# An encoder layer with routed experts: routing in two parts, two tiles' logits in another place, slots listed at another time

## The chip, the cores and the metric

The kernel runs on one core of one Trainium2 chip. The metric is the device time in microseconds of one execution of the whole program. The core has TensorE (matmuls into PSUM; PE in the profile, its weight loads PEld), VectorE (DVE), ScalarE (ACT), GpSimd (POOL) and SyncE (SP), which run their own instruction streams in order and wait for one another by semaphores; DMAs are issued from SP and from POOL.

## The reference

One layer on 1024 tokens of width 1024: two attention mixers, an output projection, then a mixture of experts, and a last norm. What the change touches is the routing of the experts:

```python
g_logits = xt @ router_group_w + router_group_b          # 4 groups
g_prob = softmax(g_logits);  g_top_p, g_top = top_k(g_prob, 1)
e_logits = xt @ router_expert_w + router_expert_b        # 4 x 8 experts
e_in_group = e_logits of the chosen group
e_top_logit, e_top = top_k(e_in_group, 2)
gates = g_top_p * softmax(e_top_logit)
expert_id = g_top * 8 + e_top                            # two experts per token
...
for each expert e:  h[tok] += gate * ((silu(x[tok] @ w_gate[e]) * (x[tok] @ w_up[e])) @ w_down[e])
```

For each expert the kernel needs two lists: which token rows it gets, and the gate of each of them.

## The kernel before

The tokens are 8 tiles of 128. The stage of interest comes after the mixers. A loop over the tiles `j` makes the second half of the output projection: `projected(j, b)` for two halves `b` of 512 columns, 12 matmuls each (L827), and VectorE's add into `q_a` (b = 0) and `h_b` (b = 1, L964). Then ScalarE squares, GpSimd makes the reciprocal root (`rstd`, L135 and L136; of `turned` for `on` and of `projected` for `xn`), VectorE writes the normed tile `xn` (L972), and SP stores it to `xn_d`. `mixed(j)` turns the next mixer tile (`on` L814, transposes L819). The routing of a tile is a generator, `routed(j)`, of which the loop takes one step after the other between the products: two groups of transposes of the new tile (L984, copied to `xt` by ScalarE), the logits (L990) and VectorE's choice of a group and of two experts (to `ohb`, L1021), the places by a product with a triangle (L1024, L1025), then the gates and the places (L1026 to L1050), and last a product that puts both into the lists (L1054): `put` has a one where a token's place is the slot, `what` holds in 32 columns each the token's number and its gate, and `first_at` in PSUM sums over all tiles. For the tiles below `JV` = 6, GpSimd makes `put` and `what`.

When the last tile is in, VectorE turns `first_at` into `rows` (L1108) and `gate` (L1109); `load_rows` gathers the rows of expert 0 from `xn_d` into `x_g` with an indirect DMA from GpSimd (L1163), TensorE transposes them (L1180), and the experts begin: 32 of them, each with 12 weight pieces of 512 KB, which are loaded 39 ahead (`load_until`), split into a high and a low part by ScalarE (`wh`) and VectorE (`wl`), and multiplied (L1196, L1220). The rows of the next expert are gathered after the sixth piece (`KR` = 5). `listed(j)` scatters each token's number and gate to `slot_d` in DRAM with two indirect DMAs (L1062); these lists are only read where an expert has more than 128 tokens.

The order of TensorE's instructions is the order in which the code stands (`manual_schedule`); that of the other engines is set by a scheduler from when it expects operands to be ready. `issue_after(x)` holds instructions back until `x` has been placed.

## Time and profile before

| | us |
|---|---|
| three runs: lowest, median, highest | 1390.99, 1392.51, 1394.03 |
| the profiled execution | 1393.38 |
| its span, first to last instruction | 1391.7 |
| last tile's add into `h_b`; the rows are ready | 745.9; 758.2 |
| first gather issued, transposes of expert 0 begin | 758.5, 763.1 |
| second gather issued, transposes of expert 1 begin | 767.8, 776.9 |

Times in the trace are microseconds from the span's start. A table by stretches gives, for each engine, its busy time in the stretch and the number of its instructions, the share of TensorE's full clock that was granted (PEclk), the mean busy share of the 16 DMA engines and their rate. A row of the timeline gives the start, the duration, the engine, the line, and what is written and read; in brackets stands how long the engine was idle just before and what ended it.

### The profile page before, as it was taken

What the parts mean: (1) busy time and instruction counts of PE and PEld (TensorE: products, weight loads), DVE (VectorE), ACT (ScalarE), POOL (GpSimd) and SP (SyncE); (2) the same over time, 40 slices, a digit from 0 to 9 for tenths busy, and PEclk for the clock granted to TensorE, in tenths of its full rate; (3) what the DMA queues carried; (4) which work ended last, traced back from release to release, by engine and by line L of the source; (5) the groups of instructions that cost most, each with busy time, mean ns of one, the idle gap of its engine ahead of it and who ended that gap; (6) DMA issues with size and microseconds to landing.
All of it is one profiled execution on the core that took longest, in us unless ns stands there. A gap on an engine that the chain in (4) does not pass through costs nothing. (4 is left out here: it accounts for less than half of the span.)

```text
span 1391.7 us, 21904 instructions
## 1 busy us (share of the span) xinstructions
PE 1303.2 (94%) x7333; PEld 1110.6 (80%) x7333; DVE 1152.4 (83%) x2001; ACT 926.2 (67%) x1366; POOL 568.6 (41%) x556
## 2 busy tenths in 40 slices
PE   5999899999998999999897999999999999999983
PEld 5999779888976889889686788878888888888862
DVE  5788997899868777667587799989999999999976
ACT  5334556655566656556443688878888888888873
POOL 5673566745566645446354611122111111111215
PEclk9999999999998999899998999999999999999997
DMA  7113321231242564445767999999999999999925
GB/s 258 62 39 85 84 68 54 61 75 36 58 138 60 145 186 117 112 128 164 278 210 240 308 371 367 353 341 372 360 351 351 345 360 355 349 353 342 376 74 226
DMA packets 213044, 299.63 MB, mean 215 GB/s; under 512 B 94307, under 2 KB 115939, under 8 KB 212928
## 3 DMA queue, kind: packets, MB, share of 16 engines
q1 hardware_dynamic: 200528, 272.91, 58.1%
q0 software_dynamic: 11968, 24.55, 6.7%
q8 instruction: 58, 0.95, 0.3%
q10 hardware_dynamic: 432, 0.75, 0.3%
q14 instruction: 58, 0.48, 0.1%
HBM read 267.85 MB, written 44.58 MB: 224 GB/s over the span
## 5 line engine op out<-in xcount | busy, mean ns | idle before, releaser
L140 DVE TENSOR_TENSOR wl<-unit,wh 128x1024 fp32r<-128x1024 f32 x140 | 168.4, 1223 | 21.1 <-ACT wh L131 20.1
L1163 POOL DMA_INDIRECT o_b<-xn_d,rows x32 | 51.4, 1606 | 303.1 <-PE ps_a L1180 300.8
L131 ACT ACTIVATE wh<-unit 128x1024 fp32r<-128x1024 f32 x140 | 147.3, 1062 | 36.3 <-PE ps_b L1196 12.5
L529 POOL TENSOR_TENSOR psum<-psum,p 128x512 f32<-128x512 f32 x93 | 138.0, 1484 | 66.7 <-ACT p L131 56.6
L263 PE MATMUL ps_i<-wih,ul 128*128 128x256 f32 x576 | 163.1, 283 | 1.2 <-DVE ul L140 1.2
L261 PE MATMUL ps_i<-wih,uh 128*128 128x256 f32 x576 | 162.7, 283 | 0.8 <-ACT uh L131 0.8
L262 PE MATMUL ps_i<-wil,uh 128*128 128x256 f32 x576 | 162.2, 282 | 0.0
L131 ACT ACTIVATE ph<-p 128x512 fp32r<-128x512 f32 x192 | 119.0, 630 | 12.7 <-DVE pl L445 5.7
L445 DVE TENSOR_TENSOR pl<-p,ph 128x512 fp32r<-128x512 f32 x93 | 96.1, 1035 | 24.7 <-ACT ph L131 24.6
L131 ACT ACTIVATE p<-ps_b 128x512 f32<-128x512 f32 x128 | 74.6, 595 | 62.2 <-PE ps_b L519 39.7
L261 PEld LDWEIGHTS ps_i<-wih,uh 128*128 128x128 f32 x576 | 109.6, 190 | 7.0 <-ACT uh L131 1.5
L262 PEld LDWEIGHTS ps_i<-wil,uh 128*128 128x128 f32 x576 | 109.4, 190 | 5.5
L263 PEld LDWEIGHTS ps_i<-wih,ul 128*128 128x128 f32 x576 | 109.5, 190 | 5.1 <-DVE ul L140 1.7
L696 POOL TENSOR_TENSOR pl<-p,ph 128x512 fp32r<-128x512 f32 x64 | 83.4, 1309 | 73.2 <-ACT ph L131 51.9
L1233 POOL DMA_INDIRECT y_d<-y,rows x31 | 50.3, 1622 | 137.5 <-ACT y L131 134.2
L140 DVE TENSOR_TENSOR wl<-rawc,wh 128x1024 fp32r<-128x1024 f32 x70 | 84.4, 1223 | 10.4 <-ACT wh L131 9.9
L500 DVE TENSOR_REDUCE m<-ps_x 128x1 f32<-128x512 f32 x128 | 84.9, 678 | 7.9 <-PE ps_x L499 7.6
L1196 PE MATMUL ps_b<-wh,x_hi 128*128 128x512 f32 x256 | 87.0, 421 | 0.0
L131 ACT ACTIVATE wh<-rawc 128x1024 fp32r<-128x1024 f32 x70 | 74.3, 1067 | 18.2 <-PE ps_b L1196 7.2
L1220 PE MATMUL ps_d<-wh,h_hi 128*128 128x512 f32 x256 | 81.0, 397 | 1.7 <-ACT h_hi L131 1.7
L1220 PE MATMUL ps_d<-wh,h_lo 128*128 128x512 f32 x256 | 81.1, 398 | 1.5 <-DVE h_lo L140 1.5
L1196 PE MATMUL ps_c<-wh,x_hi 128*128 128x512 f32 x256 | 80.9, 397 | 0.0
(326 smaller groups left out, 3888.9 us busy)
## 6 DMA issues: line engine op xcount, KB each, us to landing
unit<-in_w_up SPq DMA_DIRECT2D x49, 512.0 KB
unit<-in_w_gate SPq DMA_DIRECT2D x47, 512.0 KB
unit<-in_w_down SPq DMA_DIRECT2D x44, 512.0 KB
rawc<-in_w_gate SPq DMA_DIRECT2D x25, 512.0 KB
rawc<-in_w_down SPq DMA_DIRECT2D x23, 512.0 KB
rawc<-in_w_up SPq DMA_DIRECT2D x22, 512.0 KB
h_b<-in_w_down SPq DMA_DIRECT2D x19, 512.0 KB
raw<-in_w_in SPq DMA_DIRECT2D x36, 256.0 KB
```

The lines of the kernel that those rows point to most:

```text
L131: A.activation(o, i, f, **kw)
L140: (eng or V).tensor_tensor(lo, src, hi, op=OP.subtract)
L261: T.matmul(ps[:, jj], u_hi[j][:, k], wh, start=(k == 0 and jj == 0), stop=False, skip_group_check=True)
L262: T.matmul(ps[:, jj], u_hi[j][:, k], wl, start=False, stop=False, skip_group_check=True)
L263: T.matmul(ps[:, jj], u_lo[j][:, k], wh, start=False, stop=(k == 7), skip_group_check=True)
L445: engine("pl").tensor_tensor(pl, p, ph, op=OP.subtract)
L500: V.tensor_reduce(m2[:, j, b:b + 1], ps, axis=AX.X, op=OP.max)
L529: engine("s").tensor_tensor(st["s"], st["s"], p, op=OP.add)
L696: G.tensor_tensor(pl, p, ph, op=OP.subtract)
L1163: gathers.append(G.indirect_dma_start(out=x_g, out_offset=None, in_=xn_d[:, :], in_offset=bass.IndirectOffsetOnAxis(ap=rows, axis=0), boun ...
L1196: T.matmul(st["gu"[n % 2]], lhs[:, k % 4], rhs[:, 512 * a:512 * a + 512], start=(k == 0 and i == 0), stop=(k == 7 and i == 2))
L1220: T.matmul(py[b], lhs[:, k], w[n][:, 512 * b:512 * b + 512], start=(k == 0 and i == 0), stop=(k == 3 and i == 2))
```

## The change

Routing is cut in two. First only what the rows need: the places, `put` and `what` with the token's number alone (now all on VectorE), and a product of 32 columns (L1051 in the new numbering). Then the gates: two `Exp`, the reciprocals, `gates` on GpSimd for the tiles below 6, and a second product of 32 columns with the same `put` (L1074). The logits of tile 6 stand inside the last product of tile 7, those of tile 7 in two halves, the first ahead of the transposes of its second half. `rows` is made as soon as the first products of tile 7 are in; the gates of tiles 6 and 7 follow after it. `listed(e - 2)` stands in the loop of the experts for e = 2 to 9, with no `issue_after` round it, and `list_blocks` moves from expert 8 to expert 10.

```diff
-            run(half_product(1, o, ps, b))
+            for k, _ in enumerate(half_product(1, o, ps, b)):
+                if k == 1 and between:
+                    between()
...
+            def logits(ks):
+                if not lp:
+                    lp.append(bank("c", [P, 36]))
+                for k in ks:
+                    T.matmul(lp[0], xt[:, k], wr[:, k], start=(k == 0), stop=(k == 7))
...
+                if j == NT - 1 and b == 0:
+                    logits(range(4))
+                    yield
+            logits(range(4 if j == NT - 1 else 0, 8))
...
             T.matmul(pc, trib, ob, start=True, stop=False)
             T.matmul(pc, oneb, cum, start=False, stop=True)
+            puts = []
+            for k in range(2):
+
+                what = wo2.tile([P, NE], F32, name="what")
+                V.tensor_scalar(what, oh[:, k], r[:, 10:11], None, op0=OP.mult)
+                tmp = wo2.tile([P, NE], F32, name="tmp")
+                V.scalar_tensor_tensor(tmp, pc, 1.0, oh[:, k], op0=OP.mult, op1=OP.mult,
+                                       accum_out=r[:, 12 + k:13 + k])
+                put = wo2.tile([P, P], F32, name="put", bufs=4)
+                V.tensor_scalar(put, slots, r[:, 12 + k:13 + k], None, op0=OP.is_equal)
+                puts.append((put, what))
             V.tensor_tensor(cum, cum, ob, op=OP.add)
+            yield
+            for k, (put, what) in enumerate(puts):
+                T.matmul(first_at[:, 0:NE], put, what, start=(j == 0 and k == 0), stop=False, skip_group_check=True)
+            yield
...
+            gates = wo2.tile([P, 2, NE], F32, name="gates")
             for k in range(2):
-                put = wo2.tile([P, P], F32, name="put")
-                (V if j >= JV else G).tensor_scalar(put, slots, r[:, 12 + k:13 + k], None, op0=OP.is_equal)
-                what = wo2.tile([P, 2, NE], F32, name="what")
-                for n, col in enumerate((10, 8 + k)):
-                    (V if j >= JV else G).tensor_scalar(what[:, n], oh[:, k], r[:, col:col + 1], None, op0=OP.mult)
-                puts.append((put, what))
+                (V if j >= JV else G).tensor_scalar(gates[:, k], oh[:, k], r[:, 8 + k:9 + k], None, op0=OP.mult)
...
-            for k, (put, what) in enumerate(puts):
-                T.matmul(first_at, put, what.rearrange("p a b -> p (a b)"), start=(j == 0 and k == 0),
+            for k, (put, _) in enumerate(puts):
+                T.matmul(first_at[:, NE:2 * NE], put, gates[:, k], start=False,
                          stop=(j == NT - 1 and k == 1), skip_group_check=True)
...
+            for j, n in ((NT - 1, 1), (NT - 2, 1), (NT - 1, 1), (NT - 2, 1), (NT - 1, 3)):
                 for _ in range(n):
                     next(routes[j])
+            rows_all = lst.tile([P, 2 * NE], I32, name="rows")
+            rows = rows_all[:, 0:NE]
+            found = V.tensor_scalar(rows_all, first_at, -1.0, float(S), op0=OP.mult, op1=OP.add).ins
+            with tc.issue_after(found):
+                for j in (NT - 2, NT - 1):
+                    for _ in range(2):
+                        next(routes[j])
...
         with tc.issue_after(gathers[0]):
             load_until(NU, G)
-            for e in range(NT):
-                listed(e)
...
+            if 2 <= e < NT + 2:
+                listed(e - 2)
-            if e == NT:
+            if e == NT + 2:
                 list_blocks()
```

GpSimd, one iteration of the routing loop (j = 5) and the steps that follow, before; the two pairs of `ss` are the `rstd` of `on` for tile 7 and of `xn` for tile 5:

```order
L1045 TENSOR_SCALAR what<-oh,r 128x32 x4
L1049 COPY ents<-r 128x2
L1042 TENSOR_SCALAR put<-mats,r 128x128 x2
L135 TENSOR_SCALAR ss_9111<-ss_9111 128x1
L136 TENSOR_TENSOR ss_9111<-ss_9111,mats 128x1
L135 TENSOR_SCALAR ss_8894<-ss_8894 128x1
L136 TENSOR_TENSOR ss_8894<-ss_8894,mats 128x1
```

and the same place now, for tile 3's gates and list:

```order
L1066 TENSOR_SCALAR gates<-oh,r 128x32 x2
L1069 COPY ents<-r 128x2
L1082 DMA slot_d_75<-ents 32768x2
L1082 DMA slot_d_76<-ents 32768x2
L135 TENSOR_SCALAR ss_9113<-ss_9113 128x1
L135 TENSOR_SCALAR ss_8902<-ss_8902 128x1
L136 TENSOR_TENSOR ss_9113<-ss_9113,mats 128x1
L136 TENSOR_TENSOR ss_8902<-ss_8902,mats 128x1
```

`put` has left GpSimd, and the two scatters of a tile's list stand where it stood, ahead of both `rstd`; the program has such a pair in the loop for each of tiles 0 to 5.

GpSimd at the end of the routing, now (`ss_9179` is the `rstd` of tile 7, L1190 the gather of an expert's rows, before L1163):

```order
L1082 DMA slot_d_75<-ents 32768x2
L1082 DMA slot_d_76<-ents 32768x2
L135 TENSOR_SCALAR ss_9179<-ss_9179 128x1
L136 TENSOR_TENSOR ss_9179<-ss_9179,mats 128x1
L1190 DMA o_b_4962<-xn_d,rows 128x1024
L905 DMA rawb<-in_w_down 128x1024
L905 DMA rawb<-in_w_gate 128x2x512
...
L1069 COPY ents<-r 128x2 x2
L1082 DMA slot_d_73<-ents 32768x2
L1082 DMA slot_d_74<-ents 32768x2
...
L1190 DMA o_b_4962<-xn_d,rows 128x1024 x3
```

Tile 5's two scatters stand ahead of tile 7's `rstd`, and between the first gather and the second there are the weight loads and the scatters of tiles 6 and 7, four in all (the fence leaves out a repeated load and the second pair); before, four scatters stood there too, and twelve behind the second gather.

TensorE from the last product of tile 7 to expert 0, before:

```order
L1024 LDWEIGHTS trib
L1024 MATMUL ps_i_9218<-ohb,trib 128x32
...
L984 MATMUL ps_b<-mats,q_a 128x128 x4
L990 MATMUL ps_d<-wr,xt 128x36 x8
L1054 MATMUL ps_i_8326<-what,put 128x64 x2
L984 MATMUL ps_b<-mats,h_b 128x128 x4
L990 MATMUL ps_d<-wr,xt 128x36 x8
```

and now (L994 is the logits, L999 the transposes, `ps_i_9277` tile 5's places):

```order
L994 MATMUL ps_d<-wr,xt 128x36 x8
L827 MATMUL ps_x<-woh,o_hi 128x512
...
L999 MATMUL ps_b<-mats,q_a 128x128 x4
...
L1035 MATMUL ps_i_9277<-ohb,trib 128x32
...
L1051 MATMUL ps_i_8326<-what,put 128x32 x2
L1074 MATMUL ps_i_8326<-gates,put 128x32 x2
L994 MATMUL ps_d<-wr,xt 128x36 x4
...
L1035 MATMUL ps_i_9317<-ohb,trib 128x32
...
L999 MATMUL ps_b<-mats,h_b 128x128 x4
L1051 MATMUL ps_i_8326<-what,put 128x32 x2
L994 MATMUL ps_d<-wr,xt 128x36 x4
```

The eight logits of tile 6 moved from behind the last product into the middle of it, those of tile 7 are two halves, and the product into the lists is two.

## Rows read from the trace of the kernel before

**Rows 1.** The page: busy time, share of the span and instructions of TensorE.

```profile
PE 1303.2 (94%) x7333; PEld 1110.6 (80%) x7333; DVE 1152.4 (83%) x2001; ACT 926.2 (67%) x1366; POOL 568.6 (41%) x556
```

**Rows 2.** Stretches: from:to, length, busy time (instructions) by engine, PEclk, DMA share, GB/s.

```profile
740.00:750.00 10.00, 9.99 (x69) 8.61 (x67) 7.32 (x37) 4.15 (x13) 3.51 (x9) 1.00 0.62 202
750.00:760.00 10.00, 3.74 (x20) 3.08 (x20) 8.27 (x67) 2.69 (x6) 1.91 (x4) 0.63 0.68 262
760.00:770.00 10.00, 6.93 (x27) 5.70 (x28) 6.08 (x7) 4.84 (x7) 7.31 (x8) 0.69 0.93 327
770.00:780.00 10.00, 7.28 (x30) 5.84 (x29) 6.04 (x6) 4.37 (x5) 5.66 (x5) 0.83 1.01 298
```

**Rows 3.** Timeline: the first two experts' transposes, and the second gather's issue.

```profile
763.07 1.94 PE L1180 MATMUL ps_a<-mats,o_b 128*128 128x128 f32 x8 [5.12 <-DMA o_b<-xn_d,rows]
...
767.78 1.05 POOL L1163 DMA_INDIRECT o_b<-xn_d,rows  x1 [0.30 <-issue]
...
776.91 1.94 PE L1180 MATMUL ps_a<-mats,o_b 128*128 128x128 f32 x8 [2.72 <-DMA o_b<-xn_d,rows]
```

**Rows 4.** Timeline of one iteration of the routing loop (tile 5 to tile 6).

```profile
727.38 0.69 DVE L964 TENSOR_TENSOR h_b<-ps_x,h_b 128x512 f32<-128x512 f32 x1 [0.30 <-PE ps_x L827]
...
727.72 1.87 PE L990 MATMUL ps_d<-wr,xt 128*128 128x36 f32 x16
...
729.43 0.64 PE L1054 MATMUL ps_i<-what,put 128*128 128x64 f32 x4
...
729.65 0.19 POOL L135 TENSOR_SCALAR ss<-ss 128x1 f32<-128x1 f32 x1
...
729.88 0.48 PE L827 MATMUL ps_x<-woh,o_hi 128*128 128x512 f32 x1
...
730.55 0.75 DVE L814 SCALAR_TENSOR_TENSOR on<-o_b,ss,g_o 128x512 f32<-128x512 f32 x1
...
732.02 0.75 DVE L972 SCALAR_TENSOR_TENSOR xn<-q_a,ss,g 128x512 f32<-128x512 f32 x1 [0.59 <-POOL ss L136]
...
734.09 0.18 DVE L1007 TENSOR_TENSOR le<-lg,e 128x32 f32<-128x32 f32 x1
...
735.03 0.39 DVE L1019 TENSOR_SCALAR oh<-mats,r 128x32 f32<-128x32 f32 x2
...
735.45 0.22 DVE L1021 TENSOR_TENSOR ohb<-oh 128x32 bf16<-128x32 f32 x1
...
736.63 0.69 DVE L964 TENSOR_TENSOR h_b<-ps_x,h_b 128x512 f32<-128x512 f32 x1 [0.30 <-PE ps_x L827]
```

**Rows 5.** Timeline: VectorE's add of tile 2.

```profile
699.64 0.69 DVE L964 TENSOR_TENSOR h_b<-ps_x,h_b 128x512 f32<-128x512 f32 x1
```

**Rows 6.** Timeline from tile 7's add to the first gather.

```profile
745.87 0.69 DVE L964 TENSOR_TENSOR h_b<-ps_x,h_b 128x512 f32<-128x512 f32 x1 [0.62 <-PE ps_x L827]
...
748.41 0.57 POOL L136 TENSOR_TENSOR ss<-ss,mats 128x1 f32<-128x1 f32 x1
...
751.04 0.22 DVE L994 SCALAR_TENSOR_TENSOR lg<-ps_d,ss,br 128x4 f32<-128x4 f32 x1
...
754.15 0.48 DVE L1042 TENSOR_SCALAR put<-mats,r 128x128 f32<-128x128 f32 x2
...
755.47 0.18 DVE L1021 TENSOR_TENSOR ohb<-oh 128x32 bf16<-128x32 f32 x1
...
757.98 0.19 DVE L1108 TENSOR_SCALAR rows<-ps_i 128x32 int32<-128x32 f32 x1 [0.71 <-PE ps_i L1054]
...
758.46 1.17 POOL L1163 DMA_INDIRECT o_b<-xn_d,rows  x1 [1.91 <-DVE gate L1109]
...
759.20 3.50 DVE L140 TENSOR_TENSOR wl<-unit,wh 128x1024 fp32r<-128x1024 f32 x3 [0.93 <-ACT wh L131]
```

**Rows 7.** The list scatters: busy and mean ns, idle before; then min/median/max ns.

```profile
L1062 POOL DMA_INDIRECT slot_d<-ents x16 | 20.2, 1261 | 8.2 <-issue 4.6 <-DMA slot_d<-ents 3.7
...
L1062 POOL DMA_INDIRECT slot_d<-ents x16: 968/1085/1967, 761.8 to 791.3; - x16
```

More of the change, by code (lines that the diff above doesn't have):

```diff
@@ L953, in mixed, with projected @@
             tiles[j] = turned(o_b[j // 2][:, j % 2], 1, "a")
-        def projected(j, b):
+        def projected(j, b, between=None):
             o = tiles[j]
@@ L980, in routed @@
             xt = wo2.tile([P, 8, P], F32, name="xt", bufs=1)
+            ss = news[j][0]
+            lg = wo2.tile([P, 4 + 4 + 32], F32, name="lg")
+            V.memset(lg[:, 4:8], NEG)
+            r = wo2.tile([P, 16], F32, name="r")
+            V.tensor_scalar(r[:, 10:11], small[:, 35:36], -1.0, float(S - P * j), op0=OP.mult, op1=OP.add)
+            lp = []
+            def logits(ks):
[3 more added lines that the diff above has]
+                    T.matmul(lp[0], xt[:, k], wr[:, k], start=(k == 0), stop=(k == 7))
             for b in range(2):
@@ L986, in routed @@
                 yield
-            ss = news[j][0]
-            ps = bank("c", [P, 36])
-            for k in range(8):
-                T.matmul(ps, xt[:, k], wr[:, k], start=(k == 0), stop=(k == 7))
-            lg = wo2.tile([P, 4 + 4 + 32], F32, name="lg")
-            V.memset(lg[:, 4:8], NEG)
+                if j == NT - 1 and b == 0:
+                    logits(range(4))
+                    yield
+            logits(range(4 if j == NT - 1 else 0, 8))
+            ps = lp[0]
             for a, b in ((0, 4), (4, 36)):
@@ L998, in routed @@
             V.max_index(at, top, lg[:, 0:8])
-            r = wo2.tile([P, 16], F32, name="r")
             e4 = wo2.tile([P, 8], F32, name="e4")
-            V.tensor_scalar(r[:, 0:1], top[:, 0:1], -1.0, None, op0=OP.mult)
-            act(e4[:, 0:4], lg[:, 0:4], AF.Exp, bias=r[:, 0:1], accum_out=r[:, 1:2])
             V.tensor_copy(r[:, 3:4], at[:, 0:1])
@@ L1075, in tile_encoder @@
                     next(routes[j - 1])
-                if (MID == 0 or j == 0) and j + 1 < NT:
-                    mixed(j + 1)
-                if MID != 2 and j > 1:
-                    next(routes[j - 2])
-                projected(j, 1)
-                if MID == 2 and j > 1:
-                    next(routes[j - 2])
-                if j + 1 < NT:
-                    if MID and j:
-                        mixed(j + 1)
-                else:
-                    next(routes[j])
-                if j:
+                if j == 0:
+                    mixed(1)
+                if j < NT - 1:
+                    projected(j, 1)
+                else:
+                    projected(j, 1, lambda: next(routes[NT - 2]))
+                    next(routes[j])
+                if j > 1:
+                    next(routes[j - 2])
+                if j and j + 1 < NT:
+                    mixed(j + 1)
+                if j and j < NT - 1:
                     next(routes[j - 1])
                 if j > 1:
-                    next(routes[j - 2])
+                    for _ in range(3):
+                        next(routes[j - 2])
                 if j and j % 2 == 0:
                     load_until(RC + 3 * j // 2 - 1)
-            for j, n in ((NT - 1, 2), (NT - 2, 2), (NT - 1, 2)):
+            for j, n in ((NT - 1, 1), (NT - 2, 1), (NT - 1, 1), (NT - 2, 1), (NT - 1, 3)):
                 for _ in range(n):
                     next(routes[j])
+            rows_all = lst.tile([P, 2 * NE], I32, name="rows")
[4 more added lines that the diff above has]
+                    for _ in range(2):
+                        next(routes[j])
         x_g = o_b[0].rearrange("p a f -> p (a f)")
@@ L1105, in tile_encoder @@
                 load_until(NU)
-        rows = lst.tile([P, NE], I32, name="rows")
         gate = lst.tile([P, NE], F32, name="gate")
-        V.tensor_scalar(rows, first_at[:, 0:NE], -1.0, float(S), op0=OP.mult, op1=OP.add)
         V.tensor_copy(gate, first_at[:, NE:2 * NE])
```

9 lines of the change are left out of this document (3 added, 6 removed).

## The prediction

> **What bounds the kernel now.** I read the page's first line, then a table by stretches, then TensorE's waits, then the instructions in order of time around the one place where TensorE stands still. TensorE is busy 94% of the span [rows 1]. By stretches [rows 2] it is full at the end of the routing stage (740 to 750: 9.99 of 10 us), so this stage runs at TensorE's pace; behind it, from 750 to 780, it works 3.74, 6.93 and 7.28 of 10 us at a granted clock of 0.63 to 0.83 of 2.4 GHz. What TensorE waits for there longest are the gathers of the first two experts' rows, 5.12 and 2.72 us [rows 3]. The gather of expert 0 needs the row numbers, and these need the routing of the last tile. So the change works on the right stretch: a chain from tile 7's add to the gather. In an iteration of the routing loop I call X the start of VectorE's add into `h_b`; two of them stand at 727.38 and 736.63, so one tile takes 9.25 us [rows 4]. In the trace X is 699.64 for tile 2 [rows 5] and 745.87 for tile 7 [rows 6].
>
> **What the change really moves.** The program order says something that the change's words don't. The scatters of `listed` stood under an explicit "after the first gather"; now they stand free, and the scheduler has put those of tiles 0 to 5 into the routing loop, two per tile, on GpSimd, ahead of the `rstd` steps (L135, L136) of that iteration. Only tiles 6 and 7 are still listed between the first and the second gather: four scatters, as many as before. So the second gather is not freed of anything, and the loop gets new work in the one engine that `on` and `xn` wait for.
>
> **Part 1: TensorE's passes in the loop.** The last product of a tile was one pair of 64 columns; now there are two pairs of 32. A pair is 4 passes and takes 729.43 to 729.88, 0.45 us [rows 4]; the logits' 16 passes of 36 columns take 727.72 to 729.43, 0.107 us each, so a pass costs the same at fewer columns and the second pair costs 0.43 us. TensorE is the loop's bound, so the period's floor goes from 9.25 to 9.68.
>
> **Part 2: the lists in the loop.** Now VectorE makes the two `put` (0.48 us for both [rows 6]) and two more `what`; GpSimd is rid of its two `put` and four `what`. The index that a scatter needs is ready at about X+1.5: add 0.6, `tmp` and `cum` 0.35, `put` 0.48, `ents` about 0.1. Before, the loop's first `rstd` started at 729.65, X+2.3. Now two scatters go first. No trace row shows one in the loop; the nearest are the sixteen after the gather: mean 1.261 us, shortest 0.968 and longest 1.967, with about 0.3 us idle before each [rows 7]. I take the mean, since it falls between a median of 1.085 and the longest and the first of a pair may be a long one: 2 x 1.56 = 3.1, so `rstd` starts at X+4.65. `on` started 0.90 after it (729.65 to 730.55 [rows 4]); with one more L135 between, 1.2: X+5.9. VectorE works in order, so what follows waits: `on` 0.75, `oh` 0.39, two `xn` 1.42, three small ones 0.65, the add into `q_a` 0.69, four short ones 0.7, together 4.6 us by their durations and 4.1 by their starts, which overlap a little [rows 4]. The next add comes at X+10.0. Before, `xn` waited only 0.59 us for `rstd` and the cover was the wait for TensorE. With a scatter of d us the period is 7.5 + 2d: 9.4 for the shortest (then TensorE's 9.68 stands), 10.0 for the mean, 11.4 for the longest. The four periods from tile 2 to tile 6: 4 x (10.05 - 9.25) = **+3.2** (ends +1.7 and +8.8). Ahead of that VectorE's two extra `what` in iteration 1, where the add at 699.64 follows VectorE's own work without a wait [rows 5]: **+0.4**.
>
> **Part 3: logits in another place.** From tile 6 to tile 7 TensorE gets tile 6's logits, 1.71 us, in the middle of the last product, and one second pair, 0.43: **+2.2** for X of tile 7. This is no gain by itself; it pays only if tile 7's own chain is shorter.
>
> **Part 4: from X of tile 7 to the rows.** Before: 745.87 to 757.98, 12.1 us [rows 6], with tile 6's chain in between the links of tile 7's; the logits' use at 751.04 is 6.9 us ahead of the rows. Now tile 7's chain runs alone: from the logits' use to `le` about 1.3, an estimate from six such short steps; from `le` to the end of `ohb` 1.6, as at 734.09 to 735.67 [rows 4], and one `what` more; from there to the rows 2.0, where it was 755.65 to 757.98 with other work in between [rows 6]: 5.0 us, a gain of 1.9. But the logits start late. TensorE has them at about X+5.8. `rstd` of tile 7 stands behind tile 5's two scatters, whose index comes at X+1.9: scatters to X+4.9, `rstd` 0.85 (0.19 and 0.57 with a gap, to 748.98 before) to X+5.85, then `xn` 1.4 ahead of the logits on VectorE: X+7.25. Rows at X+12.2: **+0.1**. On GpSimd the first gather itself is queued behind these; it comes 0.3 us after the rows as before. Its other condition, the store of `xn`, is issued some 5 us ahead of it; that is longer than the first gather itself took from issue to use, 4.6, so I let it cost nothing.
>
> **Part 5: from the rows to the second gather.** The gates' chain is now behind the rows on VectorE, 20 small instructions, two `Exp` and TensorE's last pairs, about 4.3 us, and the first three `wl`, 3.50 us (from 759.20 before, 1.2 after the rows [rows 6]), stand behind it: they end about 8.0 after the rows, when `x_lo` would be due at about 6.9, 1.8 after the transposes begin (763.07 before [rows 3]). `x_lo` comes about 1.2 us late, and the GpSimd copies of the gates put the four scatters about 0.4 later. TensorE's loss of 1.2 falls into its wait of 2.7 us for the second gather [rows 3], so only the 0.4 counts: **+0.4**. If that cover were gone, it would be 1.2. In the experts TensorE is full and the rest of the lists is gone from GpSimd, which had nothing waiting there: 0.
>
> **The sum.** 0.4 + 3.2 + 2.2 + 0.1 + 0.4 = +6.3 us. The profiled execution has a span of 1391.7 and took 1393.38, so 1398.0 and 1399.7; it lies 0.9 above the median of the three runs, 1392.51, on which I forecast 1398.8.
>
> **The rivals.** (a) *The lists are hidden*: a scatter takes 1.0 or less and `rstd` never binds. Then 0.4 + 1.7 + 2.2 - 1.3 (rows at X+10.8) + 0.4 = +3.4: 1395.9. For it: the median is 1.085 [rows 7], with which the period is already 9.7; against it, the mean. (b) *Scatters in the loop are slow*: d = 1.97 as in the longest. Period 11.4, four times +2.2 = 8.8; 0.4 more ahead of tile 7, 1.5 more in its chain: 0.4 + 8.8 + 2.6 + 1.5 + 0.4 = +13.7: 1406.2. For it: VectorE is busy 7.32 of 10 us in the loop's last stretch [rows 2] and gets more to do. The Trainium skill, "SBUF — State Buffer", section "Who interferes with whom", speaks for it too: a GpSimd operation, and with it the making of a DMA's descriptors there, is shut out of a port pair for the whole of a VectorE `tensor_scalar` or copy in a two-port mode, and the moved `put` are `tensor_scalar`. No row here shows whether they held it; the spread of 0.97 to 1.97 is what the rule would look like. (c) *Not slower*: the second gather no longer lands late. The first took 4.6 us from issue to use (758.46 to 763.07), the second 9.1 (767.78 to 776.91) [rows 3, 6]. If it were 4.6 now, TensorE would go on when it is itself ready, 1.2 late, and the 2.7 us wait would be gone: -1.6 in place of +0.4. With (a) this gives +1.4: 1393.9, no change that can be told. It decides from a landing within about 7 us. Against it: the three weight loads and four scatters ahead of it on the same queue are the same. Were the lists really issued from the third expert on, this would be the likely case; the program order rules that out.
>
> **How the numbers follow.** Forecast 0.60, (a) 0.14, (b) 0.16, (c) 0.10. About 0.2%, 2.8 us, is what a measurement of this kernel can tell from no change. Faster by more: 0.05 (part of (c), with a cheaper loop than I can argue). Within: 0.13 ((c)'s rest and the low side of (a)). Slower: 0.82. The range reaches from (c)'s upper side to (b): 1394.3 to 1406.0.
>
> **What would show it.** In the profile after: scatters of `slot_d` between the `rstd` steps in the routing loop; VectorE's `on` or `xn` waiting 1 to 2 us for `rstd`; a distance between the adds into `h_b` near 10.0 us from tile 2 to tile 6 (9.7 would be (a), over 11 (b)) and 11.4 to tile 7; idle time of TensorE inside the loop, which there is none of now; 12 us from tile 7's add to the rows; the second gather still waited for. I am wrong if the period stays at 9.25, if tile 7's add-to-rows distance falls below 11, or if the wait for the second gather vanishes.

## The result: slower by 0.6 to 0.7%

| | before | changed |
|---|---|---|
| runs: lowest, median, highest (us) | 1390.99, 1392.89, 1394.03 | 1400.34, 1404.18, 1407.20 |
| the profiled execution; its span | 1393.38; 1391.7 | 1400.34; 1398.6 |
| tile 2's add; tile 6's; tile 7's | 699.64; 736.63; 745.87 | 699.16; 737.99; 749.48 |
| rows ready; first gather issued | 757.98; 758.46 | 761.67; 763.13 |
| transposes of expert 0; of expert 1 | 763.07; 776.91 | 767.61; 781.95 |
| fourth gather issued | 797.03 | 800.62 |

The ratio is 1.0072, 95% interval 1.0046 to 1.0097. The changed kernel's profiled execution was its fastest of four, so the spans differ by only 6.9 us where the two medians differ by 11.3, which is 0.8%. TensorE's line of the page and the stretches that answer [rows 1, 2] (from:to, length, busy time and instructions by engine, PEclk, DMA share, GB/s):

```profile
PE 1314.3 (94%) x7365; PEld 1120.5 (80%) x7365; DVE 1154.7 (83%) x2025; ACT 925.2 (66%) x1366; POOL 550.2 (39%) x532
...
740.00:750.00 10.00, 9.91 (x64) 8.62 (x63) 7.19 (x40) 2.43 (x8) 3.65 (x7) 1.00 0.63 240
750.00:760.00 10.00, 6.02 (x36) 5.63 (x36) 7.15 (x47) 1.77 (x4) 2.81 (x4) 0.63 0.81 237
760.00:770.00 10.00, 4.92 (x20) 4.28 (x20) 5.65 (x33) 4.31 (x11) 6.10 (x8) 0.50 0.70 253
770.00:780.00 10.00, 9.41 (x28) 7.07 (x29) 6.04 (x7) 4.71 (x5) 3.95 (x3) 0.68 0.90 302
```

TensorE is still full at the end of the loop. From 750 to 780 it is busy for longer than before (6.02, 4.92 and 9.41 us against 3.74, 6.93 and 7.28), but from 760 to 780 at a lower granted clock, 0.50 (1.2 of 2.4 GHz) and 0.68 against 0.69 and 0.83. The stretches do not hold the same work in both kernels, since the changed one is already 3.6 us late there. One iteration of the loop, which answers [rows 4] (start, duration, engine, line, what is written and read; in brackets the idle time before, and what ended it):

```profile
728.28 0.69 DVE L966 TENSOR_TENSOR h_b<-ps_x,h_b 128x512 f32<-128x512 f32 x1
...
728.62 1.87 PE L994 MATMUL ps_d<-wr,xt 128*128 128x36 f32 x16
730.33 0.61 PE L1051 MATMUL ps_i<-what,put 128*128 128x32 f32 x4
730.77 0.61 PE L1074 MATMUL ps_i<-gates,put 128*128 128x32 f32 x4
...
730.52 1.09 POOL L1082 DMA_INDIRECT slot_d<-ents  x1 [1.42 <-issue]
731.91 0.97 POOL L1082 DMA_INDIRECT slot_d<-ents  x1 [0.30 <-issue]
732.96 0.46 POOL L135 TENSOR_SCALAR ss<-ss 128x1 f32<-128x1 f32 x2
...
734.10 0.75 DVE L814 SCALAR_TENSOR_TENSOR on<-o_b,ss,g_o 128x512 f32<-128x512 f32 x1 [1.22 <-POOL ss L136]
...
737.99 0.69 DVE L966 TENSOR_TENSOR h_b<-ps_x,h_b 128x512 f32<-128x512 f32 x1
```

The second pair is there (L1074), the two scatters stand ahead of `rstd`, and `on` waits 1.22 us for it. The period is 9.71 us where it was 9.25. The end of the routing and the start of the experts, which answers [rows 3, 6]:

```profile
749.48 0.69 DVE L966 TENSOR_TENSOR h_b<-ps_x,h_b 128x512 f32<-128x512 f32 x1
750.98 0.63 PE L1051 MATMUL ps_i<-what,put 128*128 128x32 f32 x4 [1.06 <-DVE put L1046]
754.86 1.49 PE L994 MATMUL ps_d<-wr,xt 128*128 128x36 f32 x6
755.27 0.75 DVE L974 SCALAR_TENSOR_TENSOR xn<-q_a,ss,g 128x512 f32<-128x512 f32 x1 [1.20 <-POOL ss L136]
756.71 0.37 SPq L975 DMA_DIRECT2D xn_d<-xn  x1
756.82 0.38 DVE L1008 SCALAR_TENSOR_TENSOR lg<-ps_d,ss,br 128x4 f32<-128x4 f32 x2
761.67 0.22 DVE L1121 TENSOR_SCALAR rows<-ps_i 128x64 int32<-128x64 f32 x1 [0.85 <-PE ps_i L1051]
763.13 1.13 POOL L1190 DMA_INDIRECT o_b<-xn_d,rows  x1 [7.90 <-DVE r L1060]
766.19 0.32 POOL L1069 COPY ents<-r 128x2 f32<-128x2 f32 x2
766.55 2.95 ACT L131 ACTIVATE wh<-unit 128x1024 fp32r<-128x1024 f32 x3 [3.64 <-POOL ents L1069]
767.61 1.94 PE L1207 MATMUL ps_a<-mats,o_b 128*128 128x128 f32 x8 [1.98 <-DMA o_b<-xn_d,rows]
767.64 3.49 DVE L140 TENSOR_TENSOR wl<-unit,wh 128x1024 fp32r<-128x1024 f32 x3 [1.77 <-ACT wh L131]
771.05 1.28 DVE L140 TENSOR_TENSOR x_lo<-ps_a,x_hi 128x512 fp32r<-128x512 f32 x2
771.78 1.22 PE L1223 MATMUL ps_b<-wh,x_lo 128*128 128x512 f32 x2 [0.51 <-DVE x_lo L140]
781.95 1.04 PE L1207 MATMUL ps_a<-mats,o_b 128*128 128x128 f32 x8
```

Four things are to be seen. Tile 7's logits end on TensorE at 756.78 (the row above shows six of their last eight passes), behind a wait of 1.06 us for tile 5's `put`, which VectorE makes behind tile 7's add. The first gather stands 1.46 us behind the rows, where it was 0.48. ScalarE's first three `wh` of the experts wait until GpSimd's copy of `ents` (766.19) is done, which is queued behind that gather and three weight loads; so `wl` and `x_lo` are late and TensorE waits for them. And expert 1's transposes no longer wait for their gather.

Behind the fourth gather the changed kernel is 3.6 us later than before; at the end it is 6.9. Of the missing 3.3, 3.1 lie at two places where TensorE waits equally long in both kernels, but only in the changed one the granted clock falls behind the wait: 2.72 us at the block lists, and two waits of 1.0 and 1.1 close together in the last expert. First the block lists, before and changed (each fence one kernel; from the wait on, and the stretch behind it):

```profile
930.97 0.16 PE L1134 MATMUL ps_a<-fullb,trib 128*128 128x2 bf16 x1 [2.72 <-DVE mrow L1142]
...
931.07 0.71 PE L1196 MATMUL ps_b<-wh,x_hi 128*128 128x512 f32 x2
931.62 0.63 PE L1196 MATMUL ps_b<-wh,x_lo 128*128 128x512 f32 x2
...
932.00:936.00 4.00, 4.00 (x21) 3.26 (x20) 2.44 (x3) 3.08 (x4) 0.99 (x1) 1.00 0.92 255
```

```profile
970.94 0.16 PE L1161 MATMUL ps_a<-fullb,trib 128*128 128x2 bf16 x1 [2.72 <-DVE mrow L1169]
...
971.04 1.20 PE L1223 MATMUL ps_b<-wh,x_hi 128*128 128x512 f32 x2
972.04 1.05 PE L1223 MATMUL ps_b<-wh,x_lo 128*128 128x512 f32 x2
...
972.00:976.00 4.00, 4.00 (x16) 3.21 (x15) 1.23 (x1) 1.86 (x2) 0.97 (x1) 0.70 0.97 307
```

A pair of matmuls takes 1.05 us in place of 0.63 until the clock is back, and the step from one gather to the next over this place is 22.80 us (964.25 to 987.05) where before has 21.26 (924.28 to 945.54): 1.5 more. In the last expert the two last additions of rows into `y_d` lie 17.28 us apart (1337.15, 1354.43) where before has 15.74 (1331.94, 1347.68): 1.5 more.

### The profile page after: what moved, and what is told of

Its sections match the earlier page's. It is cut to its first block, busy times and chain, and to the rows that moved or that the text cites. A ratio compares the mean times of both kernels' runs of the same rounds, so it can differ in the third digit from the quotient of the medians.

```text
span 1398.6 us, 21985 instructions
## 1 busy us (share of the span) xinstructions
PE 1314.3 (94%) x7365; PEld 1120.5 (80%) x7365; DVE 1154.7 (83%) x2025; ACT 925.2 (66%) x1366; POOL 550.2 (39%) x532
## 5 line engine op out<-in xcount | busy, mean ns | idle before, releaser
L1190 POOL DMA_INDIRECT o_b<-xn_d,rows x32 | 51.9, 1622 | 348.8 <-PE ps_a L1207 340.5
L140 DVE TENSOR_TENSOR wl<-unit,wh 128x1024 fp32r<-128x1024 f32 x140 | 168.3, 1222 | 22.4 <-ACT wh L131 21.2
L445 DVE TENSOR_TENSOR pl<-p,ph 128x512 fp32r<-128x512 f32 x93 | 92.9, 1000 | 25.5 <-ACT ph L131 25.4
L140 DVE TENSOR_TENSOR wl<-rawc,wh 128x1024 fp32r<-128x1024 f32 x70 | 84.6, 1223 | 13.7 <-ACT wh L131 13.4
L1223 PE MATMUL ps_b<-wh,x_lo 128*128 128x512 f32 x256 | 82.0, 402 | 0.5 <-DVE x_lo L140 0.5
```

What stands on the lines that cost most here:

```text
L140: (eng or V).tensor_tensor(lo, src, hi, op=OP.subtract)
L445: engine("pl").tensor_tensor(pl, p, ph, op=OP.subtract)
L1190: gathers.append(G.indirect_dma_start(out=x_g, out_offset=None, in_=xn_d[:, :], in_offset=bass.IndirectOffsetOnAxis(ap=rows, axis=0), boun ...
L1223: T.matmul(st["gu"[n % 2]], lhs[:, k % 4], rhs[:, 512 * a:512 * a + 512], start=(k == 0 and i == 0), stop=(k == 7 and i == 2))
```

## The experiments

Each ratio below is to the kernel before in executions made alongside, where its median was 1393.5 to 1396.7. The instructions ahead of the routing are the same in all kernels here, yet tile 2's add lies anywhere from 696.1 to 705.1 us in their profiles, and the granted clock falls at other places of the attention stages from one execution to the next (from 414 and again from 428 us on in before, from 424 on in the changed kernel). So I compare stretches that begin at tile 2's add (VectorE's row of `h_b`), in us; the last column is the span less that add's start. "Fourth gather" counts GpSimd's gathers (`o_b<-xn_d,rows`) from the first.

| kernel | tile 2 to 6 | 6 to 7 | 7 to rows | rows to first gather | first to fourth | tile 2 to fourth | tile 2 to end |
|---|---|---|---|---|---|---|---|
| before | 36.99 | 9.24 | 12.11 | 0.48 | 38.57 | 97.39 | 692.1 |
| before again (e0) | 37.01 | 9.26 | 12.11 | 0.48 | 35.72 | 94.58 | 689.3 |
| changed | 38.83 | 11.49 | 12.19 | 1.46 | 37.49 | 101.46 | 699.4 |
| changed again (e1) | 38.83 | 11.48 | 12.11 | 1.92 | 37.38 | 101.72 | 699.6 |
| changed, lists late (e2) | 38.83 | 11.48 | 12.50 | 0.52 | 37.92 | 101.25 | 700.4 |
| changed, one pair (e3) | 38.64 | 10.73 | 11.98 | 1.38 | 38.00 | 100.73 | 697.1 |
| before, lists free (e4) | 37.02 | 9.25 | 13.57 | 3.58 | 38.65 | 102.07 | 699.7 |
| changed, one pair, lists late (e5) | 37.01 | 11.04 | 12.52 | 0.51 | 37.14 | 98.22 | 696.0 |
| before, lists late (e6) | 37.02 | 9.25 | 12.12 | 0.48 | 34.23 | 93.10 | 689.4 |
| the same again (e11) | 36.98 | 9.25 | 12.10 | 0.48 | 34.35 | 93.16 | 689.5 |
| the same, block lists at the eighth (e8) | 37.02 | 9.25 | 12.13 | 0.48 | 34.08 | 92.96 | 689.3 |
| changed, block lists at the eighth (e7) | 38.82 | 11.49 | 12.36 | 1.20 | 37.48 | 101.35 | 696.2 |
| before, logits moved (e9) | 36.98 | 11.05 | 13.64 | 0.48 | 36.36 | 98.51 | 693.3 |
| before, split routing (e10) | 38.80 | 9.70 | 11.92 | 0.51 | 38.23 | 99.16 | 696.1 |

### The two kernels again (e1, e0)

No edit. Expected of the changed kernel:

> The changed kernel once more, nothing edited. Theory T (formed on the trace after): the routing stage repeats to 0.3 us (distance of the adds into h_b from tile 2 to tile 6 38.8 us, tile 6 to tile 7 11.5, rows 12.2 behind tile 7's add, first gather 1.4 behind the rows), and the two later losses of 1.5 us each, where the granted clock fell behind a wait of TensorE that the kernel before has too (2.7 us at the block lists, 2.2 us in the last expert), come and go from one execution to the next: at least one of the two places reads 1.00 this time, or the clock falls at a third. Rival R: these two falls belong to the change (the block lists stand two experts later), and both come again at the same places. Median ratio to the kernel before 1.005 to 1.010 by either.

Measured: ratio 1.0058, interval 1.0039 to 1.0078, median 1405.03. The routing stage repeats to 0.1 us, only the first gather stands 1.92 behind the rows. Both later falls of the clock came again at the same places (the steps are 22.71 and 17.28 us), so theory T is refuted on this point. The kernel before:

> The kernel before once more, nothing edited, for a second profile. In every profile so far of a kernel that makes the block lists two experts later (five of five) the granted clock fell to 0.5 behind TensorE's 2.7 us wait there, and TensorE's next products took 1.3 to 1.7 us longer; in the one profile of before it stayed at 1.00. Theory T (chance): the fall can come here too, or not. Rival R (it belongs to the later place): it stays at 1.00 behind this wait. By both the routing stage repeats: 37.0 us from tile 2's add to tile 6's, 97.4 from tile 2's add to the issue of the fourth gather, to 0.5 us.

Measured: 1391.73 us in one run. The clock stayed at 1.00 behind both waits (steps of 21.24 and 15.74). But the routing stage did not repeat to 0.5 us as both expected: the second gather came sooner here, and TensorE waited 1.12 us for it:

```profile
776.63 1.07 PE L1180 MATMUL ps_a<-mats,o_b 128*128 128x128 f32 x8 [1.12 <-DMA o_b<-xn_d,rows]
```

In the profile ahead of the prediction that wait was 2.72, and the clock fell behind it [rows 2, 3]. So before has 689.3 to 692.1 us from tile 2's add on, the changed kernel 699.4 to 699.6: 7.4 to 10.2 more.

### The scatters held back (e2)

```diff
             if 2 <= e < NT + 2:
-                listed(e - 2)
+                with tc.issue_after(gathers[e + 1]):
+                    listed(e - 2)
```

> The changed kernel with the scatters of the lists really held back: those of tile e-2 behind expert e+1's gather, for e from 2 to 9. Theory T: in the loop TensorE's own work is the bound (9.7 us a tile), so tile 2 to tile 6 stays at 38.8 us; GpSimd is free earlier, rstd and xn of tile 7 come 1 to 1.5 us earlier, the store of tile 7's rows lands before the row numbers are there, and the first gather stands 0.5 behind the rows in place of 1.46: 1.0 us gained in all; the second gather is issued 5 us earlier, which gains nothing, since TensorE no longer waits for it. Rival P (the prediction's step): the scatters hold rstd, on and xn back and with them the loop: tile 2 to tile 6 falls by 1 us or more, and rows come 1.4 us earlier behind tile 7's add: 3 us gained.

Measured: ratio 1.0052, interval 1.0030 to 1.0074. Without a scatter in it the loop is as long as with them:

```profile
730.54 0.69 DVE L966 TENSOR_TENSOR h_b<-ps_x,h_b 128x512 f32<-128x512 f32 x1 [0.57 <-PE ps_x L827]
740.25 0.69 DVE L966 TENSOR_TENSOR h_b<-ps_x,h_b 128x512 f32<-128x512 f32 x1 [0.56 <-PE ps_x L827]
...
759.38 0.38 DVE L1008 SCALAR_TENSOR_TENSOR lg<-ps_d,ss,br 128x4 f32<-128x4 f32 x2 [2.67 <-PE ps_d L994]
...
764.75 1.17 POOL L1190 DMA_INDIRECT o_b<-xn_d,rows  x1 [10.19 <-DVE r L1055]
```

VectorE now waits 0.56 us a tile for TensorE's product, and the period stays 9.71. The rows come no earlier behind tile 7's add (12.50), though `rstd` and `xn` of tile 7 are no longer behind scatters: TensorE's logits bound that chain, and `lg` waits 2.67 us for them (759.38). The first gather moves to 0.52 us behind the rows. Theory T holds but for the size: 0.2 to 0.5 up to the fourth gather in place of 1.0. The rows come 0.3 later behind the add, and from the first gather to the fourth it takes 0.4 to 0.5 more than in the changed kernel's profiles; the wait of `wh` for `ents` is still there.

### One pair again, and both edits (e3, e5)

```diff
-            for k, (put, what) in enumerate(puts):
-                T.matmul(first_at[:, 0:NE], put, what, start=(j == 0 and k == 0), stop=False, skip_group_check=True)
+            for k, (put, what) in enumerate(puts if j >= NT - 2 else []):
+                T.matmul(first_at[:, 0:NE], put, what[:, 0], start=False, stop=False, skip_group_check=True)
...
+                if j < NT - 2:
+                    T.matmul(first_at, put, what.rearrange("p a b -> p (a b)"), start=(j == 0 and k == 0),
+                             stop=False, skip_group_check=True)
+                else:
```

> The changed kernel with one pair of 64 columns again for tiles 0 to 5 (rows and gates together), two pairs for tiles 6 and 7 alone; the lists stay in the loop. Theory T: the second pair is all that lengthened the loop, TensorE is its bound: tile 2 to tile 6 falls from 38.8 to 37.0 us, 1.8 gained in the loop, and TensorE stays full. Rival P (the prediction's step): the chain through the scatters on GpSimd and on, xn, the adds on VectorE is as long as the period itself (scatters from X+2.2 to X+4.6, on at X+5.8, 3.9 more to the next add, without a wait), so tile 2 to tile 6 stays above 38.3 and TensorE gets idle time in the loop, 0.4 us or more a tile: under 0.5 gained.

Measured: ratio 1.0059, interval 1.0036 to 1.0082. The loop gets only 0.2 us shorter in four tiles; TensorE now stands still 0.2 us in each:

```profile
733.93 0.69 DVE L966 TENSOR_TENSOR h_b<-ps_x,h_b 128x512 f32<-128x512 f32 x1
...
733.46 0.18 PE L1035 MATMUL ps_i<-ohb,trib 128*128 128x32 bf16 x1 [0.20 <-DVE ohb L1032]
...
739.74 0.75 DVE L814 SCALAR_TENSOR_TENSOR on<-o_b,ss,g_o 128x512 f32<-128x512 f32 x1 [1.25 <-POOL ss L136]
...
743.54 0.68 DVE L966 TENSOR_TENSOR h_b<-ps_x,h_b 128x512 f32<-128x512 f32 x1
```

The period is 9.61: rival P's mechanism, the chain through the scatters, `rstd` and `on`, is the bound here. Together with the last experiment this says that two bounds of nearly one length lie side by side, 9.70 by TensorE's two pairs and 9.61 by the scatters. Then both edits together must give the 1.8 us back:

> Both edits of the two experiments together: the changed kernel with one pair of 64 columns for tiles 0 to 5, and the scatters held back behind the experts' gathers. Theory T2 (two bounds of nearly one length in the loop, TensorE's two pairs with 9.7 us a tile and the chain through the scatters with 9.65, so that taking away either alone gave 0 to 0.2): now tile 2 to tile 6 falls to 37.0 us, tile 6 to tile 7 stays at 10.7, rows 12 behind tile 7's add, the first gather 0.5 behind them, no wait for the second gather: 97.9 us from tile 2's add to the fourth gather's issue, 3.6 less than the changed kernel and 0.5 more than before. Rival: there is a third bound of the same length (VectorE, which got the two put and two what), and the loop stays above 38.

Measured: ratio 1.0034, interval 1.0018 to 1.0051. Tile 2 to tile 6 is 37.01, as T2 says, and 98.22 to the fourth gather (97.9 expected).

### The lists alone (e4)

```diff
         with tc.issue_after(gathers[0]):
             load_until(NU, G)
-            for e in range(NT):
-                listed(e)
...
+            if 2 <= e < NT + 2:
+                listed(e - 2)
-            if e == NT:
+            if e == NT + 2:
                 list_blocks()
```

> The kernel before with the lists alone changed: no longer behind the first gather, listed from the third expert on in the text (so that the scheduler puts tiles 0 to 5 into the loop), block lists two experts later; one pair of 64 columns, put and what on GpSimd, logits where they were. GpSimd has its two put ahead of the two scatters here, so they end near X+4.9 (two of 1.03 us and 0.3 between, from X+2.5), rstd at X+5.0, on at X+6.1 and the next add about 3.4 later: a period of 9.5 in place of 9.25. Theory T: tile 2 to tile 6 37.0 to 38.0 us, the median 0.5 to 2 us above the kernel before. Rival P, with the 1.26 us that a scatter took behind the gather: 10.0 a tile, 3 us or more. Rival H (hidden altogether): 37.0, and the second gather, issued just as late, still makes TensorE wait 2 to 3 us; no difference.

Measured: ratio 1.0062, interval 1.0038 to 1.0087. In the loop H holds: 37.02, the scatters are hidden. They are hidden although `on` comes at X+5.99 here (732.97, X being 726.98), no sooner than in e3 (X+5.81). The difference lies behind `on`: `oh` and `ohb` stand ahead of it here and GpSimd makes `what`, so the next add follows 3.27 us after it, 0.41 of them a wait for TensorE; in e3 it follows 3.80 us after it. So the scatters lengthen the loop only together with VectorE's new work and order. But no theory had the end. Here the scatters of tiles 6 and 7 also stand ahead of the first gather:

```profile
760.57 1.77 POOL L1062 DMA_INDIRECT slot_d<-ents  x1 [0.30 <-issue]
762.64 2.06 POOL L1163 DMA_INDIRECT o_b<-xn_d,rows  x1 [0.30 <-DVE wl L140]
...
770.30 1.94 PE L1180 MATMUL ps_a<-mats,o_b 128*128 128x128 f32 x8 [11.28 <-DMA o_b<-xn_d,rows]
```

The gather comes 3.58 us behind the rows and TensorE waits 11.28 us for it. Part of that comes back, since the second gather is then not waited for; 4.7 to 7.5 stay up to the fourth gather. The changed kernel is spared this, because its gates of tiles 6 and 7 are held behind the rows.

### The lists late, on the kernel before (e6, e11, e8)

The last diff, with `with tc.issue_after(gathers[e + 1]):` around `listed(e - 2)`.

> The kernel before with the lists alone changed, and really held back: the scatters of tile e-2 behind expert e+1's gather, for e from 2 to 9, the block lists two experts later; everything ahead of the first gather as before. Theory T2: routing as before (37.0 us from tile 2's add to tile 6's, first gather 58.8 after tile 2's add); the second gather is issued as soon as the first expert's transposes have read the rows, 2.2 us behind their start instead of 4.7, and lands before TensorE wants it, so the wait of 2.7 us goes, and with it the clock's fall behind it (1.4): 93.3 to 95 us from tile 2's add to the fourth gather's issue, 2.5 to 4 less than before; the median 0.1% to 0.3% below before. Rival C: TensorE starts the second expert earlier but its clock is then low for longer, and less than 1 us stays; median within 0.2% of before.

Measured: ratio 0.9975, interval 0.9954 to 0.9995, median 1392.06. The second gather is issued right behind the first expert's transposes, and the second transposes start without a wait:

```profile
759.67 1.94 PE L1180 MATMUL ps_a<-mats,o_b 128*128 128x128 f32 x8 [5.17 <-DMA o_b<-xn_d,rows]
...
761.89 1.07 POOL L1163 DMA_INDIRECT o_b<-xn_d,rows  x1 [3.82 <-PE ps_a L1180]
...
770.57 1.03 PE L1180 MATMUL ps_a<-mats,o_b 128*128 128x128 f32 x8
```

10.90 us lie between the two groups of transposes, where before has 13.84 and 12.39. T2 holds. Once more:

> The kernel before with held-back lists and the block lists behind the tenth expert, once more, nothing edited, since its sister with the block lists behind the eighth expert was only 0.07% below the kernel before where it was 0.25%. Theory T2: the routing stage up to the fourth gather repeats (93.1 us from tile 2's add to the fourth gather's issue, no wait of TensorE for the second gather), the step over the block lists is 21.2 or 22.8 us, 687.8 or 689.4 us from tile 2's add to the end; the kernel before has 94.6 or 97.4 and 689.3 or 692.1 there, so the median is 0 to 3 us, 0 to 0.25%, below before. Rival: the 0.25% was scatter of the stages ahead of the routing, and the median is level with before or above.

Measured: ratio 0.9981, interval 0.9966 to 0.9997. Both intervals end just below 1, so this version is some 0.2% faster than the kernel before, and so faster than the changed one. From tile 2's add to the end its profiles are no shorter than the second profile of before (689.4 and 689.5 against 689.3): the 1.4 us it is ahead at the fourth gather go behind the block lists, where the clock fell (steps of 22.81). With the block lists at the eighth expert (`listed(e)` for e below 8):

> The version with the held-back lists on the kernel before, now with tile e's scatters behind expert e+1's gather for e from 0 to 7, and the block lists behind the eighth expert as in the kernel before; routing untouched. Theory T2/R (the second gather comes early, 93.1 us from tile 2's add to the fourth gather's issue; the clock falls behind the block lists' wait at the tenth expert, in seven of seven profiles, and not at the eighth, in three of three): the step over the block lists is 21.25 us and not 22.8, 687.8 us from tile 2's add to the end, against 689.4 with the block lists two experts later and 689.3 and 692.1 in the two profiles of before; median 0.3% to 0.4% below before. Rival: the clock falls at the eighth expert too once the times ahead of it have moved; then 689.4, and nothing is gained over the last one (0.25% below before).

Measured: ratio 0.9993, interval 0.9979 to 1.0007: no difference. The clock fell there too (step of 22.79); the rival is right.

### The place of the block lists (e7)

```diff
-            if 2 <= e < NT + 2:
-                listed(e - 2)
-            if e == NT + 2:
+            if e < NT:
+                listed(e)
+            if e == NT:
                 list_blocks()
```

> The changed kernel with the block lists made where the kernel before makes them, behind the eighth expert and not the tenth (the lists are listed from the first expert on in the text; the scheduler puts them into the same places as in the changed kernel). Rival R: the granted clock stays at 1.00 behind TensorE's 2.7 us wait there, near 935 us, and the median is 1.5 us below the changed kernel's 1405.0. Theory T: the fall comes and goes whatever the place, the median stays within what the runs scatter. By both the routing stage as in the changed kernel: 38.8, 11.5, 12.2 us and 101.6 from tile 2's add to the fourth gather's issue.

Measured: ratio 1.0026, interval 1.0007 to 1.0046, median 1399.08. The clock stayed at 1.00 behind this wait (step of 21.26), and also in the last expert (15.75); from tile 2's add to the end it is 3.2 to 3.4 us less than the changed kernel. Rival R's signs are there, but e8 above takes its reason away: with the lists late the eighth place has the fall too.

### The other two parts alone (e9, e10)

```diff
-                projected(j, 1)
+                projected(j, 1, (lambda: next(routes[NT - 2])) if j == NT - 1 else None)
...
-            for j, n in ((NT - 1, 2), (NT - 2, 2), (NT - 1, 2)):
+            for j, n in ((NT - 1, 1), (NT - 2, 1), (NT - 1, 1), (NT - 2, 1), (NT - 1, 3)):
```

> The kernel before with the logits alone changed: tile 6's in the middle of tile 7's last product, tile 7's in two halves behind each half's transposes; rows and gates in one part as before, lists and block lists as before. Theory T2 (the move is paid in front and not given back): tile 6 to tile 7 9.25 + 1.7 = 10.95 us; tile 7's second half of the logits waits on TensorE behind tile 6's product and this for its put, as in the changed kernel, so rows stay 11.5 to 12.3 behind tile 7's add: the first gather 1 to 2 us later, 1 to 2 us in all. Rival (the move pays): rows 10.0 to 10.5 behind the add, so that the 1.7 come back; no difference. Tile 2 to tile 6 stays 37.0 by both.

Measured: ratio 1.0032, interval 1.0014 to 1.0049. Tile 7's add comes 1.8 us later, and the rows not earlier but 1.5 later behind it (13.64). TensorE waits for `put` of tile 5, which GpSimd makes, and then for tile 7's `ohb`:

```profile
750.91 1.01 PE L1063 MATMUL ps_i<-what,put 128*128 128x64 f32 x4 [1.16 <-POOL put L1051]
...
760.48 0.19 PE L1033 MATMUL ps_i<-ohb,trib 128*128 128x32 bf16 x1 [3.12 <-DVE ohb L1030]
```

The move costs 3.3 us to the first gather; 1.1 to 3.9 are left at the fourth. The split alone:

> The changed kernel with logits, lists and block lists as in the kernel before: only rows and gates in two parts (two pairs of 32 columns for every tile, put and what on VectorE, gates of tiles 6 and 7 behind the rows). Theory T2: tile 2 to tile 6 38.8 us (+1.8), tile 6 to tile 7 9.7 (+0.45), rows 11 behind tile 7's add (1.1 less, the gates no longer ahead); behind the rows the gates' chain stands ahead of the three wl on VectorE, x_lo comes 3.4 us behind the transposes' start instead of 1.75, and TensorE works at a granted clock of 0.5 until 15 us behind the rows instead of 8: 37 to 38 us from the first gather to the fourth, where the kernel with an early second gather had 34.2. From tile 2's add to the fourth gather 97 to 98.5, to the end 692 to 694: the median 1 to 3 us above before. Rival (the split pays, since the gates leave the chain to the rows): the first gather no later than before and no more than 36 us from it to the fourth: at or below before.

(The edit is the changed kernel with the three other pieces of its diff taken back.) Measured: ratio 1.0051, interval 1.0030 to 1.0072. The loop and tile 7 as T2 says; the rows gain only 0.2 (11.92), not 1.1. Then TensorE's first expert product waits:

```profile
770.61 1.94 PE L1202 MATMUL ps_a<-mats,o_b 128*128 128x128 f32 x8 [1.14 <-DMA o_b<-xn_d,rows]
774.34 0.31 POOL L1066 COPY ents<-r 128x2 f32<-128x2 f32 x2
774.69 2.95 ACT L131 ACTIVATE wh<-unit 128x1024 fp32r<-128x1024 f32 x3 [1.50 <-issue]
775.79 1.22 PE L1218 MATMUL ps_b<-wh,x_hi 128*128 128x512 f32 x2 [3.25 <-issue]
```

It begins 5.2 us behind the transposes' start, where before has 1.8 (763.07 to 764.89): here the first `wh` (ScalarE, 774.69) come right behind `ents` of tiles 6 and 7 (GpSimd, 774.34), as in the changed kernel, though the copy now stands behind four scatters as well. Up to the fourth gather 99.16, above the 97 to 98.5 expected, and 1.8 to 4.6 above before.

## Why the prediction was right, and where it was not

The sign came out, and the median of 1404.18 lies in the range, 5.4 above the forecast of 1398.8. +6.3 us were forecast; the spans of the two profiles give +6.9, from tile 2's add on it is 7.4 to 10.2, and the medians differ by 11.3. That the sum comes so near to the spans is luck, by two errors that cancel. Up to the fourth gather the prediction has 6.3, the two first profiles 4.1 (101.46 less 97.39: 1.84 + 2.25 + 0.08 + 0.98 to the first gather, less 1.08 behind it; against the second profile of before 6.9). Another 3.1 are the two falls of the clock, which it did not have.

- **Part 1** (second pair, floor of 9.68): right. 9.70, with TensorE full; e2 shows that this alone holds the loop.
- **Part 2** (+3.2 in the loop, +0.4 ahead): mis-sized, 1.84, and 0 ahead (tile 1's add to tile 2's: 8.68 us, 8.70 before). The mechanism is there, and up to `on` with the times that were said: `rstd` at X+4.68 (4.65 said), `on` at X+5.82 (5.9). On the way two terms cancel: a scatter took 1.03 us (1.09 and 0.97) where 1.26 was taken, but the first one starts 0.78 behind its index (which is there at 729.74) where 0.3 was taken. The term that failed is the work behind `on`: 4.1 us to the next add were said, 3.89 are in the rows above, and 3.80 in e3, where TensorE's work is not the bound. So the chain is 9.61 long and not 10.0, just under TensorE's 9.70. (With the measured scatter the prediction's own 7.5 + 2d gives 9.56, but only since its misses cancel.) For the length of the loop rival (a) was the case; its condition that `rstd` never binds was not, since `on` waits 1.22 us for it.
- **Part 3** (+2.2): right, 2.25. In e9, too, the 1.8 of it which are the logits are not given back.
- **Part 4** (+0.1): right in size, 12.19 against 12.11, but with a second bound that it did not see. The prediction had TensorE's logits done at X+5.8 and `xn` holding `lg` until X+7.25. `xn` ended at X+7.21 (756.69), as said, but TensorE only at X+7.30 (756.78), because of the 1.06 us for tile 5's `put` and the half clock behind it. e2 took the scatters away from `xn` and the rows came no sooner. The step that failed in this part is the store of `xn`, which was let to cost nothing: it is issued 5.0 us ahead of the rows (756.71) and the gather stands 6.4 behind it. The same distance is 6.1 to 6.8 in e1, e3 and e7, which have the late gather, and 8.0 or more in every kernel with the gather 0.5 behind the rows. The profile puts the store's landing 5.1 to 5.8 us behind its issue in these four (5.4 in the changed kernel, at 762.1), and the gather stands 1.0 behind that landing in each of them. That is +1.0.
- **Part 5** (+0.4, with the second gather's wait as cover): wrong in its mechanism. The wait for the second gather vanished, which the prediction named as a sign against it, and rival (c) had. Its time was eaten: `x_lo` came 3.44 us behind the transposes' start (767.61 to 771.05), where it was 1.75, 1.7 later and not 1.2, and TensorE, waiting twice for half a microsecond, worked at half its clock until 776. The cause is not the gates' chain on VectorE, which ended at 764.3, but ScalarE's `wh`, held until GpSimd's copy of `ents` at 766.19; the same row stands behind `ents` in e1, e2, e3, e5 and e7. `wh` reads nothing of `ents`; the copy is the last reader of the routing's tile `r`, whose room the experts' tiles most likely take. That the `wh` follow the copy is seen at two places of it (e10 has it four scatters later, and the `wh` with it); why they do is argued, and a kernel with the copies ahead of the gather wasn't tried. First to fourth gather comes to 37.5 us: 1.1 less than in the profile of before, 1.8 more than in its second one, and 3.3 more than in e6, which shows what an early second gather is worth.
- **Rival (b)** (slow scatters, 13.7): no. The Trainium skill, "SBUF — State Buffer", section "Who interferes with whom", was quoted for it. No run here shows such a lock in the loop, nor puts it to the test there: the scatters with `put` on VectorE took 1.09 and 0.97 us, with `put` on GpSimd (e4) 1.11 and 0.97, but VectorE's `put` ends at 729.7 and the first scatter starts at 730.52.
- **The row-and-order argument** of the prediction, that the lists are not "from the third expert on" but in the loop, with four scatters between the first two gathers, is what the trace shows; e6 is what the change's words would have given, alone, and it is some 0.2% faster than before in two measurements, while its sister e8 is level with it.

What stays open: why the clock falls behind the same 2.72 us wait in one kernel and not in another. It repeats within a kernel (changed and e1, e6 and e11; before and e0). At the tenth expert it fell in all eight profiles; at the eighth it stayed in before, e0, e7 and e9 and fell in e8, and in e10, where the wait is 3.22. In the last expert it fell in the changed kernel, e1, e2 and e4 and in no other.

## What to carry to other kernels

Code that is taken out of an "issue after" can move ahead of its text: read from the program order where it went, and which engine's next step it now stands in front of. When taking away one suspected bound gains nothing, take away the next one too before calling the first harmless; here two chains of 9.70 and 9.61 us hid one another. A small copy on a side engine that is the last reader of a stage's tiles belongs, as far as this case shows, ahead of whatever long thing is queued there, since the next stage may wait for it; no kernel here tried that.

## What was not expected of the hardware

An indirect scatter's price depends on where it stands. All sixteen of a kernel (minimum, median and maximum in ns, first and last start), in the changed kernel, where twelve are in the loop, and in e6, where all are in the experts:

```profile
L1082 POOL DMA_INDIRECT slot_d<-ents x16: 967/1072/1932, 701.5 to 772.3; - x16
```

```profile
L1062 POOL DMA_INDIRECT slot_d<-ents x16: 1095/1513/2010, 791.1 to 920.7; - x16
```

In the loop a pair took 1.09 and 0.97 us however busy the DMA engines were: the pairs at 720.8, 730.5 and 740.2 us stand in stretches with a DMA share of 0.98, 0.19 and 1.01. In the experts of e6 the first of each pair took 1.9 to 2.0 us and the second 1.1. What goes with the long ones is VectorE's `wl` (128x1024, 1.23 us each). The fourteen profiles have 224 scatters; all 69 that took over 1.2 us had a `wl` beside them for 0.6 us or more, and none of the 122 with less than 0.3 us of one took over 1.14. That the `wl` makes the difference is argued, not shown: 33 more scatters had one beside them and stayed short. If it is the `wl`, the scatters behind the gather in the kernel before, seven of them over 1.2 us, were no measure for those in the loop.

The other surprise is the clock: the same wait of TensorE, 2.72 us, costs 1.3 to 2.8 us more (steps of 22.5 to 24.1 in nine profiles) or nothing (21.2 to 21.3 in four), in kernels whose experts ahead of it all take 18.2 us.
